# Two of twelve low parts per narrow chunk moved from VectorE to GpSimd, their matmuls one half piece later, and a scatter three half pieces later

## The chip, the cores and the metric

The kernel runs on one core of one Trainium2 chip. The metric is device time in microseconds (us) of one execution. The engines are called as the profile calls them: PE is TensorE's matmuls, PEld its weight loads, DVE is VectorE, ACT is ScalarE, POOL is GpSimd, SP is SyncE, whose queue (SPq) issues the weight loads from memory.

## The reference

A decoder trunk of two layers on 256 tokens of width 1024, all in float32. Layer 0 has latent attention and a dense SwiGLU, layer 1 an mLSTM and then a mixture of experts, in which each token goes to two of eight experts. The last part takes most of the time and is what the change touches:

```python
def swiglu(h, wg, wu, wd):
    return (jax.nn.silu(h @ wg) * (h @ wu)) @ wd

for e in range(N_EXPERTS):            # N_EXPERTS = 8, D_MODEL = 1024, D_FF = 3584
    y = y + combine[..., e:e + 1] * swiglu(h, wg[e], wu[e], wd[e])
```

## The kernel before

**Split numbers.** A float32 weight is used as the sum of a high part and a low part, each in a format that PE multiplies in one pass. `split` (L204) makes both from a loaded tile: ACT casts the weight into `whi` (L221), and the engine passed as `sub`, DVE unless told otherwise, subtracts that from the weight and writes `wlo` (L225). Both inputs of this subtraction, `raw` and `whi`, lie in SBUF. Each of `whi` and `wlo` has four buffers, the loaded tiles `raw` have ten.

**Experts.** The experts are sorted by their number of tokens and dealt to eight places, even ones wide (128 token slots), odd ones narrow (64 slots). In a narrow place the high and low parts of the 64 tokens stand side by side as 128 columns, so each part of a weight is multiplied once (`mm2s`, L242: all `whi` matmuls at L245, then all `wlo` matmuls at L247); in a wide place a half piece takes six matmuls (`mm3s`, L234: L237, L238 with `whi`, L240 with `wlo`). An expert's 3584 hidden columns are worked in seven chunks of 512. `_chunks` lays the chunks of a wide and of a narrow expert alternately, 28 of each.

**Pieces.** A chunk has three weights, each loaded as two pieces of 1 MB, and each piece is split and used in two halves: twelve half pieces, four each of gate, up and down. Below, G0 to G3, U0 to U3 and D0 to D3 are the half pieces of a narrow chunk's gate, up and down. The down pieces of a chunk follow the gate and up pieces of the next chunk. The stream thus repeats: a wide chunk's gate and up (8 half pieces), the narrow chunk's down before it (4), a narrow chunk's gate and up (8), the wide chunk's down (4).

**Order.** `Stream.run` walks the half pieces. Ahead of a half piece's matmuls it splits those up to three further on (`fill`, with AHEAD = 3). `soon(n, f)` (L184) puts off `f` by half pieces: it is called after the matmuls of the n-th half piece, counting the present one when it is called from `use`. PE, DVE and ACT run their instructions in exactly the order in which this code gives them (`in_order`, L453); POOL and SP are not bound by hand. `inner` (L1275) issues the gate and up matmuls of a half piece, `summed` (L1383) closes an expert: it makes `ye_hi` and `ye_lo` of the sum and puts the four scatters (L1459: two matmuls at L1463 and one DVE addition to `xs` at L1466) one and two half pieces later. `one_hot_at` (L1227) runs on POOL once per expert from the second place on, two operations at L1232.

Of the kernel before, what the change touches and what calls it, by code (L numbers as in the profile page):

```python
# [23 lines left out]
KB = D // P  # L24
# [22 lines left out]
WIDE = (True, False, True, False, True, False, True, False)  # L47
# [39 lines left out]
def trunk(ctx: ExitStack, tc: tile.TileContext, out, rope_inv, x, positions, norm_mix, norm_ffn,  # L87
# [3 lines left out]
    nc = tc.nc  # L91
# [35 lines left out]
    def ps(tag, shape, dtype=F32):  # L127
        return psum.tile(shape, dtype, name=uniq("ps_" + tag), tag=tag, bufs=4)


    def load(src, shape, key=None):
        if key in early:
            return early.pop(key)
        n = int(np.prod(shape[1:]))
        t = weights.tile([P, 2048], F32, name=uniq("raw"), tag="raw", bufs=NB_RAW)
        v = t[:, :n]
        if len(shape) == 3:
            v = v.rearrange("p (k c) -> p k c", k=shape[1])
        nc.sync.dma_start(v, src)
        return v  # L140
# [18 lines left out]
    class Stream:  # L159
# [2 lines left out]
        def __init__(self):  # L162
            self.items, self.ready, self.later, self.at = [], [], [], 0

        def piece(self, src, shape, use, after=None, key=None):

            raw = []

            def get(j, sub):
                if not raw:  # L170
                    raw.append(load(None if key in early else src(), shape, key))
                v = raw[0]
                if isinstance(v, list):
                    return [w.rearrange("p a c -> p (a c)") for w in split(v[2 * j:2 * j + 2], sub)]
                return split(v[:, 2 * j:2 * j + 2] if shape[1] == 4 else v[:, j], sub)

            self.items.append((partial(get, 0), lambda w: use(0, w), None))
            self.items.append((partial(get, 1), lambda w: use(1, w), after))
# [25 lines left out]
    def split(v, sub=nc.vector):  # L204
        vs = v if isinstance(v, list) else [v]
        shape = [P, 2, 512] if isinstance(v, list) else list(v.shape)
        n = int(np.prod(shape[1:]))
        hi = weights.tile([P, 1024], F32R, name=uniq("whi"), tag="whi", bufs=NB_HI)[:, :n]
        lo = weights.tile([P, 1024], F32R, name=uniq("wlo"), tag="wlo", bufs=NB_LO)[:, :n]
        if len(shape) == 3:  # L210
            hi = hi.rearrange("p (k c) -> p k c", k=shape[1])
            lo = lo.rearrange("p (k c) -> p k c", k=shape[1])
        if chores and begun[0]:
            chores.pop(0)()
        with ExitStack() as order:
            if held:
                for ins in held.pop(0):
                    order.enter_context(tc.issue_after(ins))
            for i, part in enumerate(vs):
                h, l = (hi[:, i], lo[:, i]) if isinstance(v, list) else (hi, lo)  # L220
                nc.scalar.copy(h, part)  # L221
                if sub == PUT_OFF:
                    put_off.append(partial(nc.vector.tensor_sub, l, part, h.bitcast(F32)))
                elif sub:
                    sub.tensor_sub(l, part, h.bitcast(F32))  # L225
        return hi, lo
# [12 lines left out]
        for o, l, r, _, stop in terms:  # L239
            nc.tensor.matmul(o, l[0], r[1], start=False, stop=stop)  # L240

    def mm2s(terms):  # L242

        for o, l, r, start, _ in terms:
            nc.tensor.matmul(o, l, r[0], start=start, stop=False)  # L245
        for o, l, r, _, stop in terms:
            nc.tensor.matmul(o, l, r[1], start=False, stop=stop)  # L247


    ident = const([P, P], F32, "ident")  # L250
# [100 lines left out]
    def rsqrt_steps(ssq, scales, name):  # L351

        n = ssq.shape[1]
        v = tmp([P, n], F32, name + "_v")
        y = tmp([P, n], F32, name + "_y")
        t = tmp([P, n], F32, name + "_t")
        yi = y.bitcast(I32)
        steps = [partial(nc.vector.tensor_scalar, v[:, a:b], ssq[:, a:b], 1.0 / width, EPS, op0=OP.mult, op1=OP.add)
                 for a, b, width in scales]
        steps += [partial(nc.vector.tensor_scalar, yi, v.bitcast(I32), 1, None, op0=OP.logical_shift_right),  # L360
                  partial(nc.vector.tensor_scalar, yi, yi, -1.0, float(0x5F3759DF), op0=OP.mult, op1=OP.add)]
        each = [slice(i, i + 1) for i in range(n)]
        if n <= NT:
            steps.append(partial(nc.vector.tensor_scalar, v, v, -0.5, None, op0=OP.mult))
        for _ in range(3):
            if n <= NT:
                steps += [partial(nc.vector.scalar_tensor_tensor, t[:, c], y[:, c], v[:, c], y[:, c],
                                  op0=OP.mult, op1=OP.mult) for c in each]
                steps += [partial(nc.vector.scalar_tensor_tensor, y[:, c], t[:, c], 1.5, y[:, c],
                                  op0=OP.add, op1=OP.mult) for c in each]  # L370
            else:
                steps += [partial(nc.vector.scalar_tensor_tensor, t, y, -0.5, y, op0=OP.mult, op1=OP.mult),
                          partial(nc.vector.tensor_mul, t, t, v),
                          partial(nc.vector.scalar_tensor_tensor, y, t, 1.5, y, op0=OP.add, op1=OP.mult)]
        return y, steps
# [71 lines left out]
    def at(pair, *idx):  # L447
        return pair[0][idx], pair[1][idx]
# [158 lines left out]
    r, more = rsqrt_steps(ssq, [(0, NT, Q_LORA), (NT, 2 * NT, KV_LORA)], "lat")  # L607
# [25 lines left out]
    def q_rotary(wq4, b):  # L633
        p = ps("a", [P, 4, ROPE])
        for k in range(2):
            mm3(p, tok(cT, k, b), at(wq4[k], slice(None), slice(None), slice(NOPE, QK)), k == 0, k == 1)
        return p
# [7 lines left out]
    for a in range(2):  # L645
        for b in range(NT):
            nc.tensor.matmul(rows_p[:, a, b * P:(b + 1) * P], r[:, 2 * a + b:2 * a + b + 1].to_broadcast([P, P]), ident,
                             start=True, stop=True)
# [65 lines left out]
    for half in range(2):  # L714
# [6 lines left out]
        for b in range(NT):  # L721
            p = q_rotary(wq4, b) if half else qr_first[b]
# [3 lines left out]
        for h in range(hs, hs + 4, 2):  # L726
            p = ps("a", [P, 2, S])
# [6 lines left out]
        for h in range(hs, hs + 4, 2):  # L734
            p = ps("a", [P, 2, S])
# [3 lines left out]
        for b in range(NT):  # L739
            p = ps("a", [P, 4, VD])  # L740
# [52 lines left out]
    piece = []  # L793
# [60 lines left out]
    r = x_ffn.rsqrt("ffn0")  # L854
# [79 lines left out]
    for k in range(KB):  # L934
        for n in range(2):
            nc.tensor.matmul(rows_p, wg[:, k].rearrange("p a c -> p (a c)"), aT[n][:, k],
                             start=k + n == 0, stop=k == KB - 1 and n == 1)
# [35 lines left out]
    for blocks, src in ((slice(0, 2), Mr), (slice(2, 3), Mr[:, P:])):  # L973
        n = src.shape[1] // P
        src = src.rearrange("p (a c) -> p a c", a=n)
# [43 lines left out]
    for h in range(HEADS):  # L1019
        e = ps("b", [P, 3, P])  # L1020
# [3 lines left out]
                         start=False, stop=True)  # L1024
# [30 lines left out]
    r = rsqrt_pool(hsq, VD, "head")  # L1055
# [159 lines left out]
    def expert_at(n):  # L1215

        if n == 0:
            return 0
        if not numbers:
            numbers.extend(nc.values_load_multi_w_load_instructions(  # L1220
                ids[0:1, :], engines=[nc.sync.engine], min_val=0, max_val=NE - 1,
                skip_runtime_bounds_check_because="a sum of expert numbers of which one alone is taken")[1])
        return numbers[n]
# [22 lines left out]
    for h2 in range(HEADS // 2):  # L1246
        t = ps("a", [P, 2, S])
        y = tmp([P, 2, NT, VD], F32, "y")
        for j in range(2):
            h = 2 * h2 + j  # L1250
# [16 lines left out]
    def expert_chunk(e, c):  # L1267

        for w, after in ((moe_w_gate, gated), (moe_w_up, upped)):
            p = []  # L1270
            for i in range(2):
                moe.piece(lambda w=w, i=i: w[expert_at(e), c, i], [P, 4, 512], partial(inner, e, i, p),
                          partial(after, e, c, p) if i else None)

    def inner(e, i, p, j, w):  # L1275
        if i + j == 0:
            p.append(ps("a", [P, 512]))
        xg = tokens[e][0]
        k = 4 * i + 2 * j
        if not WIDE[e]:  # L1280
            mm2s([(p[0], xg[:, k + kk], at(w, slice(None), kk), k + kk == 0, k + kk == KB - 1) for kk in range(2)])
            return
        mm3s([(p[0], (xg[:, 0, k + kk], xg[:, 1, k + kk]), at(w, slice(None), kk), k + kk == 0, k + kk == KB - 1)
              for kk in range(2)])
# [98 lines left out]
    def summed(e):  # L1383

        ye = []
        for h in range(2):
            hi = tmp([P, 512], F32R, "ye_hi")
            nc.scalar.copy(hi, acc[e, h])
            ye.append([hi])
        for h in range(2):  # L1390
            lo = tmp([P, 512], F32R, "ye_lo")
            nc.vector.tensor_sub(lo, acc[e, h], ye[h][0].bitcast(F32))
            ye[h].append(lo)
        for h in range(2):
            for b in range(NT):
                moe.soon(1 + h, partial(scatter, e, h, b, ye[h]))

    def last_down(e, c):

# [68 lines left out]
    moe = Stream()  # L1468
# [109 lines left out]
    xg = bigt([P, KB, P], F32, "xg")  # L1578
    with tc.If(rv > 0):
        for e in range(NE):  # L1580
# [5 lines left out]
            for c in range(NCH):  # L1586
                gu = []
                for w in (moe_w_gate[e], moe_w_up[e]):
                    p = ps("a", [P, 512])
# [14 lines left out]
                for i in range(2):  # L1604
                    raw = load(moe_w_down[e, 2 * c + i], [P, 2, D])
                    for h in range(2):
                        for kk in range(2):
                            j = 2 * i + kk
                            nc.tensor.matmul(acc[h], hT[:, j], raw[:, kk, h * 512:(h + 1) * 512],
                                             start=c == 0 and j == 0, stop=c == NCH - 1 and j == 3)  # L1610
            for h in range(2):
                ye = tmp([P, 512], F32, "ye_hi")
                nc.scalar.copy(ye, acc[h])
                for b in range(NT):
                    p = ps("a", [P, 512])
# [61 lines left out]
```

## Time and profile before

| | |
|---|---|
| median of 3 runs | 1419.63 us (1419.06 to 1422.76) |
| profiled execution, its own time | 1419.83 us |
| its span in the trace | 1418.1 us |
| granted clock of PE over the span | 0.992 of full speed |
| stretch of the experts in the trace | about 500 to 1390 us |
| busy share of the span | PE 96%, DVE 88%, ACT 70%, POOL 6% |

The span is what the trace covers, from the first instruction to the last; 1.7 us of the profiled execution's time lie around it. Two notes for reading the rows: PE's matmuls overlap, so the shown length of one (about 0.39 us) is longer than the distance from one to the next (0.23 us); and DVE's operations overlap slightly too, so a row of eleven 1.22 us operations is shorter than eleven times that.

### The profile page before, as it was taken

To read this page: it belongs to the slowest core of one execution; us is meant where nothing else is said; L and a number is where in the kernel's file an instruction comes from. 1 tells how busy PE (TensorE), PEld (TensorE's weight loads), DVE (VectorE), ACT (ScalarE), POOL (GpSimd) and SP (SyncE) were. 2 spreads that over 40 slices of the span, in tenths; PEclk is the share of its full clock that TensorE was granted. 3 is DMA by queue.
4 is the path that set the end of the run, shared out by engine and by line. 5 is a ranking of instruction groups with operands and counts; after the bars stand their busy time and mean duration, and the time that the engine had idled before them with its cause. 6 is when DMAs were issued, how large, how long until landed. Compare 5 with 4: busy or idle time off the path is not lost.

```text
span 1418.1 us, 18971 instructions
## 1 busy us (share of the span) xinstructions
PE 1367.2 (96%) x6457; PEld 1090.4 (77%) x6457; DVE 1249.8 (88%) x1602; ACT 998.5 (70%) x1270; POOL 78.2 (6%) x112
## 2 busy tenths in 40 slices
PE   7999999999999899999999999999999999999995
PEld 5888888888887687777777878777777777777774
DVE  6959998957977898989999898999989899999996
ACT  5545444444864587878878787878878787888884
POOL 4300000000020100000000020000011000001000
PEclk9999999999999999999999999999999999999998
DMA  9455666555457598999999999999999998999970
GB/s 359 159 208 208 216 213 210 193 184 207 169 188 267 224 365 311 379 374 369 370 370 399 379 368 372 384 373 358 403 368 388 378 400 341 394 404 398 388 315 32
DMA packets 63183, 439.07 MB, mean 310 GB/s; under 512 B 7441, under 2 KB 7606, under 8 KB 11238
## 3 DMA queue, kind: packets, MB, share of 16 engines
q1 hardware_dynamic: 61190, 429.20, 78.6%
q0 software_dynamic: 1728, 8.56, 1.7%
q8 instruction: 52, 0.85, 0.2%
q14 instruction: 53, 0.43, 0.1%
q10 hardware_dynamic: 160, 0.02, 0.0%
HBM read 436.67 MB, written 1.08 MB: 309 GB/s over the span
## 4 chain that ended last, share of the span: by engine, by line
PE 81%; DVE 12%; issue 3%; ACT 2%; POOL 1%; DMA 0%; DVEq 0%; ACTq 0%; POOLq 0%
PE ps_a L237 11%; PE ps_a L238 11%; PE ps_a L240 11%; PE ps_a L247 7%; DVE wlo L225 6%; PE ps_a L245 4%; PE ps_b L237 4%; PE ps_b L238 4%; PE ps_b L240 4%; PE ps_a L1334 3%; PE ps_b L232 3%; PE ps_b L230 3%; PE ps_b L231 3%; PE ps_b L245 3%; PE ps_b L247 3%
## 5 line engine op out<-in xcount | busy, mean ns | idle before, releaser
L225 DVE TENSOR_TENSOR wlo<-raw,whi 128x1024 fp32r<-128x1024 f32 (+1 forms) x787 | 923.8, 1218 | 97.6 <-ACT whi L221 92.4
L221 ACT CAST whi<-raw 128x1024 fp32r<-128x1024 f32 (+1 forms) x796 | 801.2, 1049 | 252.3 <-PE ps_a L238 95.7
L237 PE MATMUL ps_a<-whi,xg 128*128 128x512 f32 x448 | 177.3, 396 | 1.1 <-ACT whi L221 1.1
L238 PE MATMUL ps_a<-whi,xg 128*128 128x512 f32 x448 | 175.5, 392 | 0.0
L247 PE MATMUL ps_a<-wlo,xg 128*128 128x512 f32 x448 | 153.2, 423 | 11.2 <-DVE wlo L225 11.2
L240 PE MATMUL ps_a<-wlo,xg 128*128 128x512 f32 x448 | 139.6, 393 | 1.9 <-DVE wlo L225 1.9
L245 PE MATMUL ps_a<-whi,xg 128*128 128x512 f32 x448 | 141.1, 396 | 0.0
L247 PEld LDWEIGHTS ps_a<-wlo,xg 128*128 128x128 f32 x448 | 74.5, 189 | 67.5 <-DVE wlo L225 58.6
L240 PEld LDWEIGHTS ps_a<-wlo,xg 128*128 128x128 f32 x448 | 84.0, 188 | 21.7 <-DVE wlo L225 3.2
L237 PEld LDWEIGHTS ps_a<-whi,xg 128*128 128x128 f32 x448 | 84.2, 188 | 20.0 <-ACT whi L221 1.5
L245 PEld LDWEIGHTS ps_a<-whi,xg 128*128 128x128 f32 x448 | 84.2, 189 | 19.3
L238 PEld LDWEIGHTS ps_a<-whi,xg 128*128 128x128 f32 x448 | 84.3, 188 | 18.2 <-DVE xg L1539 0.5
L237 PE MATMUL ps_b<-whi,hT_hi 128*128 128x512 f32 x224 | 90.9, 406 | 0.0
L237 PE MATMUL ps_a<-whi,xT_hi 128*128 128x512 f32 x224 | 88.6, 395 | 0.1
L238 PE MATMUL ps_a<-whi,xT_lo 128*128 128x512 f32 x224 | 88.4, 395 | 0.0
L238 PE MATMUL ps_b<-whi,hT_lo 128*128 128x512 f32 x224 | 88.1, 394 | 0.0
L785 DVE CUSTOM_DVE_ANT_0 junk<-raw,wr 128x1024 bf16<-128x1024 f32 x64 | 78.1, 1220 | 2.5 <-DMA raw<-mlstm_w_out_dram 1.9
L245 PE MATMUL ps_b<-whi,hT_hi 128*128 128x512 f32 x224 | 73.8, 409 | 0.0
L1232 POOL TENSOR_SCALAR oh<-slots,slot_at 128x128 f32<-128x128 f32 x14 | 27.5, 1970 | 815.3 <-PE ps_a L1521 392.1
L247 PE MATMUL ps_b<-wlo,hT_hi 128*128 128x512 f32 x224 | 71.6, 399 | 0.3 <-DVE wlo L225 0.3
L240 PE MATMUL ps_b<-wlo,hT_hi 128*128 128x512 f32 x224 | 70.3, 395 | 0.0
L240 PE MATMUL ps_a<-wlo,xT_hi 128*128 128x512 f32 x224 | 70.1, 393 | 0.0
(444 smaller groups left out, 1941.9 us busy)
## 6 DMA issues: line engine op xcount, KB each, us to landing
raw<-moe_w_gate_dram SPq DMA_DIRECT2D x112, 1024.0 KB, 7.2
raw<-moe_w_up_dram SPq DMA_DIRECT2D x112, 1024.0 KB, 7.3
raw<-moe_w_down_dram SPq DMA_DIRECT2D x107, 1024.0 KB, 7.3
raw<-ffn_w_gate_dram SPq DMA_DIRECT2D x14, 1024.0 KB, 4.9
raw<-ffn_w_up_dram SPq DMA_DIRECT2D x14, 1024.0 KB, 4.7
raw<-ffn_w_down_dram SPq DMA_DIRECT2D x14, 1024.0 KB, 5.0
raw<-mlstm_w_in_dram SPq DMA_DIRECT2D x12, 1024.0 KB, 4.7
raw<-mla_w_out_dram SPq DMA_DIRECT2D x4, 1024.0 KB, 7.8
```

The source lines that it names most:

```text
L221: nc.scalar.copy(h, part)
L225: sub.tensor_sub(l, part, h.bitcast(F32))
L230: nc.tensor.matmul(o, l[0], r[0], start=start, stop=False)
L231: nc.tensor.matmul(o, l[0], r[1], start=False, stop=False)
L232: nc.tensor.matmul(o, l[1], r[0], start=False, stop=stop)
L237: nc.tensor.matmul(o, l[0], r[0], start=start, stop=False)
L238: nc.tensor.matmul(o, l[1], r[0], start=False, stop=False)
L240: nc.tensor.matmul(o, l[0], r[1], start=False, stop=stop)
L245: nc.tensor.matmul(o, l, r[0], start=start, stop=False)
L247: nc.tensor.matmul(o, l, r[1], start=False, stop=stop)
L785: nc.vector.tensor_tensor_reduce(junk, a, b, 1.0, 0.0, OP.mult, OP.add, acc)
L1334: nc.tensor.matmul(t[:, n, j], src[:, j * P:(j + 1) * P], twice, start=n + j == 0, stop=n + j == 4)
```

## The change

For the gate and the up weight of a narrow chunk, the subtraction of the second half piece (G1 and U1) is issued on POOL instead of DVE, through the argument `on_pool`. The low-part matmuls of those two half pieces are put off with `moe.soon(2)`: they run after all matmuls of the next half piece (G2, U2). The four scatters of an expert come four and five half pieces after `summed` instead of one and two.

```diff
-        def piece(self, src, shape, use, after=None, key=None):
+        def piece(self, src, shape, use, after=None, key=None, on_pool=None):
...
             def get(j, sub):
+                if j == on_pool:
+                    sub = nc.gpsimd
...
-    def mm2s(terms):
+    def mm2s(terms, later=None):
 
         for o, l, r, start, _ in terms:
             nc.tensor.matmul(o, l, r[0], start=start, stop=False)
-        for o, l, r, _, stop in terms:
-            nc.tensor.matmul(o, l, r[1], start=False, stop=stop)
+
+        def low_parts():
+            for o, l, r, _, stop in terms:
+                nc.tensor.matmul(o, l, r[1], start=False, stop=stop)
+
+        later(low_parts) if later else low_parts()
...
-                          partial(after, e, c, p) if i else None)
+                          partial(after, e, c, p) if i else None, on_pool=None if WIDE[e] or i else 1)
...
-            mm2s([(p[0], xg[:, k + kk], at(w, slice(None), kk), k + kk == 0, k + kk == KB - 1) for kk in range(2)])
+
+            mm2s([(p[0], xg[:, k + kk], at(w, slice(None), kk), k + kk == 0, k + kk == KB - 1) for kk in range(2)],
+                 partial(moe.soon, 2) if (i, j) == (0, 1) else None)
...
-                moe.soon(1 + h, partial(scatter, e, h, b, ye[h]))
+                moe.soon(4 + h, partial(scatter, e, h, b, ye[h]))
```

## Rows read from the trace of the kernel before

**Rows 1.** The page, part 1: busy us, share of the span, instructions

```profile
PE 1367.2 (96%) x6457; PEld 1090.4 (77%) x6457; DVE 1249.8 (88%) x1602; ACT 998.5 (70%) x1270; POOL 78.2 (6%) x112
```

**Rows 2.** Busy time by stretch, the experts: engines, PE clock, DMA share, GB/s

```profile
500.00:1390.00 890.00, 872.38 (x4041) 688.80 (x4040) 828.16 (x822) 726.09 (x846) 28.01 (x15) 1.00 0.95 371
```

**Rows 3.** Waits, 500 to 1390: engine, line, releaser: total us, times, longest

```profile
PEld ps_a L247 <- DVE wlo L225: 58.6, 126, 1.1
ACT whi L221 <- PE ps_b L238: 53.0, 27, 2.1
DVE wlo L225 <- ACT whi L221: 43.7, 62, 1.2
PE ps_a L247 <- DVE wlo L225: 11.2, 26, 0.6
PEld ps_a L1463 <- DVE ye_lo L1392: 8.2, 6, 2.3
```

**Rows 4.** Waits of the DMA queue itself, 500 to 1390

```profile
SPq L139 <- DVE wlo L225: 696.2, 311, 6.4
```

**Rows 5.** Chain that ended last, 911 to 925: start us, us, what

```profile
911.00 0.47 PE ps_b L245 x2
911.47 0.46 PE ps_b L247 x2
...
920.74 0.47 PE ps_a L245 x2
921.21 0.66 PE ps_a L247 x2
...
924.14 0.23 PE ps_b L237
```

**Rows 6.** Timeline of DVE, 880 to 970: start us, us, operation, count, [idle before]

```profile
912.46 4.62 DVE L225 TENSOR_TENSOR wlo<-raw,whi 128x1024 fp32r<-128x1024 f32 x4
917.00 0.69 DVE L1360 TENSOR_TENSOR hT_lo<-ps_a,hT_hi 128x512 fp32r<-128x512 f32 x1
917.60 12.57 DVE L225 TENSOR_TENSOR wlo<-raw,whi 128x1024 fp32r<-128x1024 f32 x11
930.76 1.23 DVE L225 TENSOR_TENSOR wlo<-raw,whi 128x1024 fp32r<-128x1024 f32 x1 [0.59 <-ACT whi L221]
...
951.28 1.28 DVE L1392 TENSOR_TENSOR ye_lo<-ps_b,ye_hi 128x512 fp32r<-128x512 f32 x2
...
957.38 10.52 DVE L225 TENSOR_TENSOR wlo<-raw,whi 128x1024 fp32r<-128x1024 f32 x9
968.64 1.22 DVE L225 TENSOR_TENSOR wlo<-raw,whi 128x1024 fp32r<-128x1024 f32 x1 [0.73 <-ACT whi L221]
```

**Rows 7.** Timeline of ACT, 908 to 932

```profile
910.58 2.95 ACT L221 CAST whi<-raw 128x1024 fp32r<-128x1024 f32 x3 [0.30 <-PE ps_a L238]
```

**Rows 8.** Timeline of POOL, first 60 us: the two subtractions of 1024 columns

```profile
24.41 2.34 POOL L616 TENSOR_TENSOR wlo<-raw,whi 128x1024 fp32r<-128x1024 f32 x1
41.02 2.41 POOL L225 TENSOR_TENSOR wlo<-raw,whi 128x1024 fp32r<-128x1024 f32 x1
```

**Rows 9.** Timeline of DVE beside these, and line 495's lengths (ns min/median/max)

```profile
24.47 2.30 DVE L533 SCALAR_TENSOR_TENSOR mix_y<-mix_t,mix_y 128x1 f32<-128x1 f32 x1
41.33 0.67 DVE L731 TENSOR_TENSOR qkT<-ps_a,rows 128x512 f32<-128x512 f32 x1
41.93 1.65 DVE L495 TENSOR_TENSOR qr<-rope_u,rope_v 128x128 f32<-128x128 f32 x1
...
L495 DVE TENSOR_TENSOR qr<-rope_u,rope_v x8: 279/280/1803, 38.0 to 51.9; 128x128 f32<-128x128 f32 x8
```

**Rows 10.** Timeline of POOL and of DVE, 814 to 818, in the experts' stretch

```profile
814.69 2.31 POOL L1232 TENSOR_SCALAR oh<-slots,slot_at 128x128 f32<-128x128 f32 x1 [188.96 <-PE ps_a L1521]
814.26 1.22 DVE L225 TENSOR_TENSOR wlo<-raw,whi 128x1024 fp32r<-128x1024 f32 x1
815.39 2.45 DVE L225 TENSOR_TENSOR wlo<-raw,whi 128x1024 fp32r<-128x1024 f32 x2
```

## The prediction

> **What bounds the kernel now.** The page's busy shares come first [rows 1]: PE 96%, DVE 88%, POOL 6%. They suggest that DVE work could go to POOL for nothing, and that PE would then hardly gain. Shares over the span mix stages, so the second view is the stretch of the experts alone [rows 2]: in 890 us PE shows 872 busy (its matmuls overlap, so this is too high), DVE 828, and the DMA engines are busy 95% of the time. Third come the waits there [rows 3]: PE's low-part matmuls of the narrow chunks (L247) wait for DVE's `wlo` 126 times at the weight load and 26 times at the matmul, some 152 waits in 28 narrow chunks, over five in each; DVE waits for ACT's casts 43.7 us, and ACT itself waits for PE to free buffers. No wait for a DMA is among them. The DMA queue, on the other side, waits for DVE to free loaded tiles [rows 4]: loading follows the compute and doesn't limit it.
>
> So the bound changes within a pair of chunks. The chain [rows 5] shows it: a narrow half piece that PE runs freely takes 0.47 + 0.46 = 0.93 us (911.00, 911.47), but in the gate and up of the next chunk 0.47 + 0.66 = 1.13 us (920.74, 921.21), which is DVE's pace: eleven `wlo` in a row take 12.57 us, so (12.57 - 1.22) / 10 = 1.135 us from one to the next [rows 6]. There DVE has no idle time: from 912.46 to 930.17 it runs 4 `wlo`, one `hT_lo` and 11 `wlo` without a gap [rows 6]; its next idle time is 0.59 us, in the wide part, where a half piece has six matmuls and PE leads. **In the narrow gate and up DVE sets the pace; DVE's idle time lies elsewhere, and with only three half pieces split ahead it can't be used for the narrow part.** Whatever DVE's queue loses or gains between G0 and U3 reaches the end of the run nearly one to one, 28 times.
>
> **The change, part by part.**
>
> *Removed from DVE.* 2 x 28 = 56 subtractions, each worth a distance of 1.135 us on a full queue: 2.27 us a chunk, 63.6 us in all.
>
> *Added on POOL.* 56 subtractions of 1024 columns. The trace has two on POOL: 2.34 and 2.41 us [rows 8]. POOL is free in that stretch (28 us of 890, [rows 2]), so their length alone would cost nothing as long as PE gets the result in time.
>
> *What they do to DVE.* This decides, and the trace shows it in the first 60 us. Beside POOL's subtraction at 24.41 to 26.75, DVE's operation on a single column starts at 24.47 and takes 2.30 us: it ends when POOL's ends [rows 8, 9]. Beside the one at 41.02 to 43.43, L495 starts at 41.93 and takes 1.65 us, where its median is 0.28 [rows 9]; it too ends just behind POOL's. Between them L731, one of whose inputs is in PSUM, runs in 0.67 us under the same POOL operation. So a DVE operation with both inputs in SBUF stands still while POOL subtracts two SBUF tiles. Nearly all that DVE runs between G0 and U3 is `wlo<-raw,whi`, of just this kind; only `hT_lo` (0.60 us, an input from PSUM) isn't.
>
> *Who comes first.* Against a running DVE queue POOL waits: its operation at 814.69 begins under a `wlo`, takes 2.31 us, and ends 0.4 us behind the second `wlo`'s end (about 816.6), while DVE's pair from 815.39 takes 2.45 us, 0.1 more than two at the usual distance [rows 10]. I read this as: POOL is let in after the operation in flight and one more. G1's cast, the third of three from 910.58, ends at 913.53 [rows 7], when D3's subtraction is in flight (the first of four from 912.46); POOL would get in behind G0's at about 914.8, hold DVE until 917.1, and G2's `wlo` follows. U1's turn comes behind U0's in the same way; its buffer comes free only when G1's put-off low matmuls are done, which still leaves PE three half pieces.
>
> *Price.* A hold costs DVE 2.30 us [rows 9] and saves 1.135: **+1.16 us each, 2.33 a chunk, +65 us for 28.** Bounds: if G1's request falls one operation later, `hT_lo` runs under the hold and G1 costs 0.56 instead of 1.16, together 1.72 a chunk, +48 us; the longest hold, 2.41 plus the 0.1 of rows 10 for the hand-over, gives 1.37 each, +77 us. Below zero lies only the case without a hold (a rival). I take the full price, since both requests, placed by the rows, find DVE with `wlo` next.
>
> *Put-off low matmuls.* The same matmuls in another order, no cost by themselves. They keep a `wlo` buffer one half piece longer: the split four places on waits for them. For G1 that is U1 on POOL, for U1 the second half piece of the wide down on DVE. Behind that one on DVE the next `wlo` would queue, but DVE reaches it two operations after U3, when PE, at DVE's pace, has done U1. Without that cover the cost is up to one matmul group, 0.47 us a chunk (13 us in all); I take 0. PE's own need: G1's low matmuls come after G2, and G2's `wlo` on DVE is later than POOL's result, so PE waits for DVE, not for POOL.
>
> *Scatter later.* It removes PE's waits for `ye_lo` (8.2 us at six weight loads, [rows 3]). These stand behind the three narrow experts that end mid-stream. DVE there is full from `ye_lo` at 951.28 to 967.90, with its next idle time at 968.64 [rows 6], and the additions at L1466 stay in the same narrow gate and up. PE waits less for `ye_lo` and as much more for the next `wlo`. Gain between 0 and 8 us; I take 1, as DVE's full queue is the nearest row. The same move at the wide experts falls in PE's part and adds or removes no instruction: 0.
>
> *DMA and POOL's queue.* SP reloads a tile when its second half is subtracted, for the two first pieces now by POOL, some 2 to 4 us later. Ten tiles and no wait for a DMA cover this: 0. Two one-hot operations per expert share POOL's queue in one narrow chunk of seven, up to 2.3 us each [rows 10]; if they came ahead of U1, its result would be late there by up to 4.6 us in at most 4 chunks: 0 to 18 us, taken as 0, because U1's subtraction is given before them.
>
> *Sum.* 1419.83 (the profiled execution: span 1418.1 and 1.7 around it; 0.2 above the median) + 65 - 1 = **1484 us**, with 1464 (+48, -4) to 1497 (+77) for this case. PE's clock stays at 1.00 in this stretch, as PE remains busy.
>
> **The rivals.** *A, no hold for long subtractions.* The held operations seen in rows 9 are short; a pair of two 1024-column subtractions side by side is not in the trace. If DVE ran on beside POOL, it would be 2.27 us ahead per chunk, and PE's loss in the narrow part would go: four half pieces at 0.2 us (1.13 less 0.93) and some 0.6 us at the first wait, 1.4 us a chunk, 39 us: **1381 us, faster**. It decides as soon as the hold is below 1.135 us. Against it: both operations of the right kind in rows 9 end with POOL's. Chance 0.10.
>
> *B, partly covered holds.* If both holds regularly fall on a DVE operation with a PSUM input, of the size of `hT_lo` (0.60 us from its start to the next), 1.20 of the 2.33 us is covered: 1.13 x 28 = 32 us, **1450 us** (1440 to 1464, above which the forecast's own lower bound takes over). Against it: between G0 and U3 there is one such operation, and none near U1. Chance 0.08.
>
> *C, POOL is let in only when DVE pauses.* DVE would run G2, G3, U0 and U2 first. G3 starts at 917.60 in rows 6, so U2 ends at 917.60 + 3 x 1.135 + 1.22 = 922.22, less two subtractions that are gone, 919.95. There DVE must stop for a buffer, POOL runs until 922.3, and PE has stood since G2. Then PE does G1's low part (0.47), G3, U0 (0.93 each), U1's high part, U2, U1's low part and U3: U3 ends at 927.4 instead of 924.14 [rows 5], 3.3 us x 28 = 92: **1512 us**. Against it: in rows 10 POOL got in between back-to-back operations. Chance 0.06.
> The Trainium skill ("SBUF — State Buffer", section "Who interferes with whom") bears on A and C: it says that a DVE instruction with two SBUF inputs and a POOL instruction that reads SBUF exclude each other for the whole instruction, and that the order of issue decides who blocks. By that rule the trace agrees against A (2.30 us held of 2.34); for C it leaves open how long DVE's queue keeps the first place, and rows 10 alone speak.
>
> *The change does nothing* (holds just equal what they save, 1.135 us): within 4 us of 1419.8, chance 0.02.
>
> **How the numbers follow.** Forecast 0.74, A 0.10, B 0.08, C 0.06, nothing 0.02. The range takes in the forecast's bounds, B below and C's time above: 1440 to 1512, leaving out A, the null case and part of C, some 0.15. About 0.3% (4 us) is what a measurement of this kernel can tell from no change: faster 0.10, same 0.02, slower 0.88.
>
> **What would show it.** In the changed trace: POOL with 56 subtractions of 2.3 us or, with their wait for DVE, up to 4.5 us; in every narrow chunk two DVE `wlo` (G2 and U0 or U2) of up to 3.4 us instead of 1.22; PE's waits for `wlo` at L247 grown by some 60 us; DVE's idle time unchanged in sum (890 - 828 = 62 us, [rows 2]), nearly all of it in the wide parts; a pair of chunks 2.3 us longer. I am wrong if DVE's `wlo` keep 1.22 us beside POOL's (A), or if PE waits for POOL rather than DVE (C).

## The result, and the profile of the changed kernel

The changed kernel takes 1503.47 us (median of 4 runs, 1501.3 to 1506.14), the kernel before 1419.49 us: a ratio of 1.0587, 95% interval 1.0561 to 1.0614, or 84 us more. The forecast was 1484 us with a range of 1440 to 1512. The profiled execution took 1506.14 us, its span is 1504.4 us.

The page, part 1 (busy us, share of the span, instructions), against [rows 1]; then busy time by stretch, the experts, which now reach to about 1475 us, against [rows 2] (columns as there: PE, PEld, DVE, ACT, POOL, PE clock, DMA share, GB/s):

```profile
PE 1375.0 (91%) x6457; PEld 1106.1 (74%) x6457; DVE 1301.6 (87%) x1546; ACT 1005.3 (67%) x1270; POOL 245.5 (16%) x168
```

```profile
500.00:1475.00 975.00, 880.75 (x4033) 705.15 (x4031) 878.98 (x766) 731.92 (x845) 195.16 (x71) 0.98 0.92 339
```

DVE has 56 instructions fewer and POOL 56 more, as the change says. Yet DVE's busy time in the experts went up from 828 to 879 us (from 1249.8 to 1301.6 over the whole span): DVE has fewer operations, and some of them take longer. PE's clock there is 0.98 on the mean, where it was 1.00. The first 500 us are the same in both.

The waits of the same stretch, against [rows 3], and those of the DMA queue, against [rows 4]:

```profile
PEld ps_a L251 <- DVE wlo L227: 121.1, 77, 3.3
PE ps_a L251 <- DVE wlo L227: 87.1, 51, 2.9
DVE wlo L227 <- ACT whi L223: 75.1, 80, 3.1
PEld ps_a L251 <- POOL wlo L227: 4.1, 2, 2.1
```

```profile
SPq L139 <- DVE wlo L227: 719.2, 312, 6.4
SPq L139 <- POOL wlo L227: 65.4, 28, 4.2
```

(L225 and L247 of before are L227 and L251 here.) PE waits for DVE fewer times but far longer: 121.1 us at the weight loads where it was 58.6, 87.1 at the matmuls where it was 11.2. It hardly waits for POOL, twice in 56. SP waits 28 times for POOL to free a loaded tile; no engine's wait for a DMA is among the long ones.

What POOL does to DVE is seen in one narrow chunk. First POOL's timeline, then DVE's, operation by operation (start us, us), against [rows 6]:

```profile
1063.00 3.43 POOL L227 TENSOR_TENSOR wlo<-raw,whi 128x1024 fp32r<-128x1024 f32 x1 [25.60 <-ACT whi L223]
1068.44 3.04 POOL L227 TENSOR_TENSOR wlo<-raw,whi 128x1024 fp32r<-128x1024 f32 x1 [2.01 <-PE ps_a L251]
```

```profile
1064.23 3.30 DVE L227 TENSOR_TENSOR wlo<-raw,whi 128x1024 fp32r<-128x1024 f32 x1
1067.44 0.68 DVE L1368 TENSOR_TENSOR hT_lo<-ps_a,hT_hi 128x512 fp32r<-128x512 f32 x1
1068.05 1.21 DVE L227 TENSOR_TENSOR wlo<-raw,whi 128x1024 fp32r<-128x1024 f32 x1
1069.18 3.39 DVE L227 TENSOR_TENSOR wlo<-raw,whi 128x1024 fp32r<-128x1024 f32 x1
1072.49 4.62 DVE L227 TENSOR_TENSOR wlo<-raw,whi 128x1024 fp32r<-128x1024 f32 x4
```

These are G2 (3.30), `hT_lo`, G3 (1.21), U0 (3.39) and, in the last row, U2, U3 and two of the wide down. G2 begins at 1064.23, stands until POOL's G1 ends at 1066.43, and ends 1.10 us behind that; U0 likewise behind POOL's U1 (1071.48). Each is some 2.1 to 2.17 us longer than the usual 1.22. PE beside it, against [rows 5]:

```profile
1067.58 1.19 PE L251 MATMUL ps_a<-wlo,xg 128*128 128x512 f32 x4 [1.20 <-DVE wlo L227]
...
1072.62 0.72 PE L251 MATMUL ps_a<-wlo,xg 128*128 128x512 f32 x2 [2.11 <-DVE wlo L227]
1073.18 1.10 PE L247 MATMUL ps_a<-whi,xg 128*128 128x512 f32 x4
1074.11 1.10 PE L251 MATMUL ps_a<-wlo,xg 128*128 128x512 f32 x4
1075.05 0.63 PE L247 MATMUL ps_a<-whi,xg 128*128 128x512 f32 x2
1075.51 0.63 PE L251 MATMUL ps_a<-wlo,xg 128*128 128x512 f32 x2
1075.98 0.40 PE L239 MATMUL ps_b<-whi,hT_hi 128*128 128x512 f32 x1
```

The rows show two pauses, 1.20 us at G2 and 2.11 us at U0, both ended by the DVE operation that was held. From U0 on PE doesn't wait any more in this chunk. U1's subtraction holds U0 in 22 of the 28 narrow chunks of the trace.

### The profile page after: what moved, and what is told of

The parts are those of the page before. It is cut to its first block, busy times and chain, and to the rows that moved or that the text cites. A ratio compares the mean times of both kernels' runs of the same rounds, so it can differ in the third digit from the quotient of the medians.

```text
span 1504.4 us, 19073 instructions
## 1 busy us (share of the span) xinstructions
PE 1375.0 (91%) x6457; PEld 1106.1 (74%) x6457; DVE 1301.6 (87%) x1546; ACT 1005.3 (67%) x1270; POOL 245.5 (16%) x168
## 4 chain that ended last, share of the span: by engine, by line
PE 73%; DVE 15%; issue 5%; ACT 5%; POOL 1%; DMA 0%; DVEq 0%; ACTq 0%; POOLq 0%
DVE wlo L227 10%; PE ps_a L239 10%; PE ps_a L240 10%; PE ps_a L242 10%; PE ps_a L251 5%; PE ps_b L239 4%; ACT whi L223 3%; PE ps_a L247 3%; PE ps_b L242 3%; PE ps_b L240 3%; PE ps_a L1342 3%; PE ps_b L234 3%; PE ps_b L232 3%; PE ps_b L233 3%; PE ps_b L247 2%
## 5 line engine op out<-in xcount | busy, mean ns | idle before, releaser
L227 DVE TENSOR_TENSOR wlo<-raw,whi 128x1024 fp32r<-128x1024 f32 (+1 forms) x731 | 973.7, 1368 | 133.6 <-ACT whi L223 125.7
L227 POOL TENSOR_TENSOR wlo<-raw,whi 128x1024 fp32r<-128x1024 f32 (+2 forms) x62 | 180.7, 2916 | 667.4 <-ACT whi L223 570.4
L251 PE MATMUL ps_a<-wlo,xg 128*128 128x512 f32 x448 | 149.8, 438 | 91.7 <-DVE wlo L227 87.1
L251 PEld LDWEIGHTS ps_a<-wlo,xg 128*128 128x128 f32 x448 | 85.2, 205 | 140.2 <-DVE wlo L227 121.1
L242 PE MATMUL ps_a<-wlo,xg 128*128 128x512 f32 x448 | 139.4, 392 | 1.9 <-DVE wlo L227 1.9
L247 PE MATMUL ps_a<-whi,xg 128*128 128x512 f32 x448 | 140.8, 417 | 0.0
L247 PEld LDWEIGHTS ps_a<-whi,xg 128*128 128x128 f32 x448 | 89.6, 201 | 21.4
L242 PEld LDWEIGHTS ps_a<-wlo,xg 128*128 128x128 f32 x448 | 83.9, 188 | 21.7 <-DVE wlo L227 3.2
L239 PEld LDWEIGHTS ps_a<-whi,xg 128*128 128x128 f32 x448 | 84.2, 188 | 19.7 <-ACT whi L223 1.5
L240 PEld LDWEIGHTS ps_a<-whi,xg 128*128 128x128 f32 x448 | 84.2, 188 | 18.4 <-DVE xg L1547 0.5
L247 PE MATMUL ps_b<-whi,hT_hi 128*128 128x512 f32 x224 | 73.3, 407 | 0.0
L251 PE MATMUL ps_b<-wlo,hT_hi 128*128 128x512 f32 x224 | 71.0, 396 | 1.3 <-DVE wlo L227 1.3
```

Of the source, the lines that this page charges most:

```text
L239: nc.tensor.matmul(o, l[0], r[0], start=start, stop=False)
L240: nc.tensor.matmul(o, l[1], r[0], start=False, stop=False)
```

## The experiments

The theory: a POOL subtraction stops DVE's subtractions for its length, which costs time where DVE sets PE's pace. The rivals: POOL's result is late, the put-off matmuls carry the loss, or something else follows from the longer pauses.

**Take away POOL's reading (e4_write_only).** The low part of G1 and U1 is left out: POOL writes zeros instead.

```diff
...
+                elif sub is nc.gpsimd and begun_moe[0]:
+                    for _ in range(3):
+                        sub.memset(l.bitcast(F32), 0.0)
...
```

> POOL makes no subtraction for G1 and U1 but writes zeros into the same low-part tile, three times over, so it is busy about as long but reads nothing from SBUF; the low part of these half pieces is left out. Theory (DVE stands still because both engines read SBUF): no DVE subtraction over 1.4 us, DVE is ahead by two subtractions per chunk, PE's waits at the narrow low parts all but vanish, and the time falls below that of the kernel before, to about 1380 us (1370 to 1395). Rival (POOL's result is late, or the put-off matmuls and their buffers cost): time stays above 1460 us, with PE waiting for POOL.

Measured: 1387.34 us, ratio to before 0.9769 (0.9753 to 0.9785). POOL's and DVE's operations in its trace (DVE: ns min/median/max):

```profile
L229 POOL MEMSET wlo<- 128x1024 f32 x168 | 160.5, 956 | 553.0 <-PE ps_b L255 439.2 <-PE ps_a L255 46.5 <-PE ps_b L246 36.6
...
L231 DVE TENSOR_TENSOR wlo<-raw,whi x587: 1210/1220/1228, 500.8 to 1362.7; 128x1024 fp32r<-128x1024 f32 x196
```

POOL is as busy there, 160 us, but no DVE subtraction exceeds 1.228 us. 116 us separate this kernel from the changed one, and 32 us of it lie below the kernel before: I read this as what DVE's pace in the narrow chunks costs there, at the least, as the put-off is still in this kernel. It isn't a gain to keep, because the kernel leaves out 56 low parts. The memsets don't wait for ACT's cast as the subtractions do, so POOL is also earlier; since PE hardly waited for POOL in the changed kernel, that isn't where the 116 us come from. The Trainium skill ("SBUF — State Buffer", section "Who interferes with whom") says that a DVE instruction with two SBUF inputs contends with a POOL instruction that reads SBUF, not with one that only writes it; the rows of the changed kernel (3.30 and 3.39 us) agree with the first half, the rows here (at most 1.228 us) with the second.

**Move the holds to where DVE has time (e9_wide_instead).** One POOL subtraction in each wide chunk, none in the narrow ones, nothing put off, the scatter as before.

```diff
-    ... on_pool=None if WIDE[e] or i else 1)
+    ... on_pool=1 if WIDE[e] and not i and w is moe_w_up else None)
...
```

> The kernel before with one subtraction per wide chunk on POOL (the second half piece of the up weight), none in the narrow chunks, no put-off matmuls, the scatter as before. Theory (a hold costs time only where DVE sets the pace; in the wide part DVE has 1.7 to 2.2 us idle per pair, more than the 1.03 a hold costs it): 1416 to 1430 us, in spite of 28 holds of about 2.2 us. Rival (a hold costs its 0.8 to 0.95 us wherever it is): 1442 to 1447 us.

Measured: 1425.61 us, ratio 1.0036 (1.0023 to 1.0049). A subtraction in POOL's timeline there, and the one beside it in DVE's:

```profile
1043.28 2.40 POOL L227 TENSOR_TENSOR wlo<-raw,whi 128x1024 fp32r<-128x1024 f32 x1 [29.04 <-ACT whi L223]
1044.53 2.23 DVE L227 TENSOR_TENSOR wlo<-raw,whi 128x1024 fp32r<-128x1024 f32 x1 [1.21 <-ACT whi L223]
```

POOL starts 1.25 us ahead of DVE, while DVE waits for a cast. So DVE's operation is only 1.0 us longer than the usual 1.22, not the 2.2 us that I expected, and the move saves DVE 1.135 us: its busy time over the span is 1249.4 us, against 1249.8 before. The 28 subtractions cost 5 us here; one per narrow chunk costs 29 to 33 us, as the next two runs show. What this run shows is that a POOL subtraction that begins in DVE's idle time costs little. What a full hold of 2.1 us would cost in the wide part isn't shown, nor where the 5 us come from.

**One at a time (e5_gate_alone, e8_up_alone).** G1 alone, then U1 alone on POOL; both low parts stay put off and the scatter late.

```diff
-    ... on_pool=None if WIDE[e] or i else 1)
+    ... on_pool=None if WIDE[e] or i or w is moe_w_up else 1)      # e5_gate_alone
+    ... on_pool=None if WIDE[e] or i or w is moe_w_gate else 1)    # e8_up_alone
```

> The changed kernel with only G1 on POOL, U1 back on DVE. Theory: one hold of 2.17 us for a saved 1.135 at G2, after which PE follows DVE through U3, so no further loss: 1.03 us x 28 = 29 us, and few falls of PE's clock since the long pause of 2.3 us at U0 is gone: 1446 to 1456 us. Rival (every hold costs the same share of the whole loss): half of 84, 1462 us.

> The changed kernel with only U1 on POOL, G1 back on DVE. Theory: the hold at U0 costs 1.03 us, PE then runs the rest of the up weight at its own pace behind DVE, 0.55 us more, and PE's clock falls in some chunks: 1.58 us x 28 = 44, with up to 1.5 us for each fall: 1460 to 1480 us, above the gate alone by 10 to 30 us. Rival (the holds cost alike): within 5 us of the gate alone.

Measured: 1452.75 us (ratio 1.0238, 1.0221 to 1.0255) and 1448.70 us (1.0212, 1.0195 to 1.0229), so 33 and 29 us. The first lies in the theory's span. The second missed it (1460 to 1480) and is within 5 us of the first, as the rival said. The trace shows why: U1's hold fell elsewhere. POOL and DVE in that kernel, one narrow chunk:

```profile
1035.54 5.00 POOL L227 TENSOR_TENSOR wlo<-raw,whi 128x1024 fp32r<-128x1024 f32 x1 [27.48 <-ACT whi L223]
```

```profile
1035.96 2.35 DVE L227 TENSOR_TENSOR wlo<-raw,whi 128x1024 fp32r<-128x1024 f32 x2
1038.44 3.19 DVE L227 TENSOR_TENSOR wlo<-raw,whi 128x1024 fp32r<-128x1024 f32 x1
```

U0 and U2 went ahead of POOL, and U3 was held: POOL's operation took 5.00 us, 2.6 of it waiting. PE beside it, and its waits for POOL between 500 and 1420 us:

```profile
1040.60 0.73 PE L251 MATMUL ps_a<-wlo,xg 128*128 128x512 f32 x2 [1.23 <-POOL wlo L227]
```

```profile
PE ps_a L251 <- POOL wlo L227: 24.0, 20, 1.3
```

These are U1's put-off low matmuls, with only U3 behind them. So here PE waits for POOL's late result, the first rival of this section, 20 times and in spite of the put-off. Together the two singles cost 62 us; both contain the put-off of both low parts (7 us, next run), so 56 us without counting it twice, if the prices add. The changed kernel costs 84: **28 us come only from the two together**.

**The put-off alone (e2_defer_only).** DVE makes all low parts; G1's and U1's low matmuls are put off; scatter as before.

```diff
-    ... on_pool=None if WIDE[e] or i else 1)
+    ... on_pool=None)
...
-                moe.soon(4 + h, partial(scatter, e, h, b, ye[h]))
+                moe.soon(1 + h, partial(scatter, e, h, b, ye[h]))
```

> The kernel before with the put-off low matmuls of G1 and U1 alone; DVE makes all low parts, the scatter stays. Theory: the order of matmuls and the longer-held buffer cost little: 1419 to 1430 us. Rival (the put-off matmuls carry the loss): 1450 us or more.

Measured: 1426.41 us, ratio 1.0054 (1.0037 to 1.0071): 7 us, inside the theory's span.

```profile
1027.83 1.19 PE L251 MATMUL ps_a<-wlo,xg 128*128 128x512 f32 x4 [0.60 <-DVE wlo L227]
1028.86 0.63 PE L247 MATMUL ps_a<-whi,xg 128*128 128x512 f32 x2
1029.32 0.64 PE L251 MATMUL ps_a<-wlo,xg 128*128 128x512 f32 x2
```

```profile
1023.16 9.16 DVE L227 TENSOR_TENSOR wlo<-raw,whi 128x1024 fp32r<-128x1024 f32 x8
```

Behind U2's `wlo` PE has U2's and U1's low matmuls and then U3 to do, at its own pace, to 1029.79, 1.96 us from the end of its wait. In the kernel before only U2's low matmuls lay there, and U3 followed at DVE's pace, 1.135 us plus the last 0.66 us. DVE's row begins with G3 and U0 to U3, so U3 is done at 1023.16 + 4 x 1.135 + 1.22 = 1028.92, and PE ends U3's matmuls 1.04 us behind that (1029.96), where it was 0.77 before (923.37 to 924.14, [rows 5, 6]). The difference, 0.27 us a chunk, makes the 7 us.

**The change without the put-off (e12_no_put_off).**

```diff
-                 partial(moe.soon, 2) if (i, j) == (0, 1) else None)
+                 None)
```

> The changed kernel without the put-off: POOL makes G1's and U1's low parts, their matmuls come at once, the scatter stays late. Theory (POOL's result is there before the subtraction that DVE was held in, so the put-off buys nothing and costs 0.3 to 0.55 us a chunk at the end of the up weight): 8 to 15 us below the changed kernel, 1488 to 1496 us. Rival (POOL's result is late for PE, which the put-off hides): 1510 us or more, with PE waiting for POOL.

Measured: 1505.61 us, ratio to before 1.0597 (1.058 to 1.0615). Neither expectation held. PE now does wait for POOL, and PE's clock is lower still (0.96 over the stretch):

```profile
PEld ps_a L251 <- POOL wlo L227: 28.3, 25, 3.0
```

```profile
500.00:1480.00 980.00, 895.13 (x4045) 716.02 (x4044) 877.05 (x767) 729.79 (x847) 182.65 (x71) 0.96 0.89 337
```

So POOL's result is late for an immediate use, in 25 chunks, and the put-off hides it; but PE reaches the same held DVE operation anyway, and the time is the same. That isn't proof that the put-off costs nothing here: PE's clock falls to 0.50 at 21 places of the experts in this trace and at 13 in the changed kernel's, so two different sums come out alike.

**PE's clock (e6_pe_kept_busy, e10_pe_kept_busy_half).** The mean of 0.98 in the changed kernel is made of 13 short falls of 3.4 us each; the kernel before has one in the experts. Three stretches of its trace, and PE's timeline there:

```profile
1172.00:1184.50 12.50, 9.21 (x40) 6.61 (x39) 12.06 (x9) 10.04 (x13) 5.70 (x2) 1.00 0.94 335
1184.50:1187.90 3.40, 3.40 (x9) 2.65 (x9) 3.40 (x4) 1.83 (x2) 0.00 (x0) 0.50 0.90 366
1187.90:1192.00 4.10, 4.10 (x25) 3.52 (x25) 3.05 (x3) 3.43 (x4) 0.00 (x0) 1.00 1.00 396
```

```profile
1183.05 0.72 PE L251 MATMUL ps_a<-wlo,xg 128*128 128x512 f32 x2 [2.11 <-DVE wlo L227]
1183.61 1.21 PE L247 MATMUL ps_a<-whi,xg 128*128 128x512 f32 x4
1184.61 1.91 PE L251 MATMUL ps_a<-wlo,xg 128*128 128x512 f32 x4
...
1187.96 0.40 PE L239 MATMUL ps_b<-whi,hT_hi 128*128 128x512 f32 x1
```

Behind the pause of 2.11 us the granted clock falls to 0.50, the 1.2 GHz level; four matmuls that took 1.10 us in the chunk shown first take 1.91, and by 1187.90 the clock is back at 2.4 GHz. From U0's low matmuls to the wide chunk's first matmul PE takes 4.91 us here (1183.05 to 1187.96) and 3.36 us in the chunk shown first (1072.62 to 1075.98): a fall costs about 1.55 us, and the twelve more than before some 18 us, by estimate. The two kernels put matmuls of zeros into PE's pauses, which add nothing to the sums:

```diff
+            if (i, j) == ((0, 0) if up else (1, 0)):
+                def busy_then(low_parts):
+                    for _ in range(8 if up else 4):
+                        nc.tensor.matmul(p[0][:N], zerob, onesb[:, None, :].to_broadcast([P, 4, P]), start=False, stop=False)
+                    low_parts()
+                mm2s(terms, busy_then)
...
-                    for _ in range(8 if up else 4):
+                    for _ in range(4 if up else 2):      # e10_pe_kept_busy_half
```

> The changed kernel with matmuls of zeros put where PE pauses in the narrow chunk: 4 of 512 columns (bf16, 64 output rows) between G2's high and low parts, 8 between U0's, about 0.9 and 1.8 us of PE time, less than the pauses of 1.2 and 2.3 us. Theory (PE's clock falls after the pauses, 13 times in the experts' stretch, at about 1.2 to 1.6 us each): the clock stays up there and the time falls by 15 to 22 us, to 1481 to 1489 us. Rival (the clock's fall costs nothing, the holds alone make up the loss): unchanged within 4 us, or slower by what the added matmuls cost.

> The changed kernel with half as many matmuls of zeros in PE's pauses, 2 between G2's high and low parts and 4 between U0's. Theory (a fall of PE's clock costs 1 to 1.7 us, and the added matmuls of the fuller version cost some of what they saved): clock above 0.988 and 1488 to 1496 us. Rival (the falls cost little, about 5 us in all): 1497 to 1502 us whatever the clock.

Measured: 1497.99 us with the full number (ratio to before 1.0553, 1.0532 to 1.0575) and 1491.86 us with half of it (1.0509, 1.0492 to 1.0525); the mean clock is 0.99 in both, where the changed kernel has 0.98. The full version gave less than expected, 5 us below the changed kernel; the half one gave 12 us and lies in the theory's span. Their traces have one fall and two (one of them 6.8 us long) left in the experts. That the added matmuls of the full version cost what they saved is not shown: its profiled execution, at a clock of 0.993, took 1494.33 us, and the three others, at 0.992 to 0.987, took 1497.48 to 1501.72. So in this version the longer executions are those with the lower clock. **The falls cost 12 us of the 84 by e10, which leaves some in, and about 18 by the rows.**

**The scatter (e3_no_scatter_move, e1_scatter_only).** The changed kernel without the move, and the move alone.

```diff
-                moe.soon(1 + h, partial(scatter, e, h, b, ye[h]))
+                moe.soon(4 + h, partial(scatter, e, h, b, ye[h]))      # e1_scatter_only; e3 is the reverse
```

> The changed kernel with the scatters back at one and two half pieces. Theory: the move is worth little, 1503 to 1512 us. Rival (the move is needed since POOL's holds and the scatter collide): over 1512 us.

> The kernel before with the scatters three half pieces later, nothing else. Theory: DVE is full at these places, PE's wait for the sum's low part turns into waits for DVE's next subtractions: 1415 to 1420 us. Rival (PE's waits of 14.5 us there are real losses): 1405 to 1411 us.

Measured: 1503.67 us, no different from the changed kernel, and 1417.70 us, ratio 0.9983 (0.9973 to 0.9994), 2 us below before.

**Lead (e7_four_ahead, e11_five_ahead).** If the narrow chunks are bound by DVE for want of lead, more lead must help the kernel before, without POOL. (The kernel gives each number a line of its own.)

```diff
-NB_RAW, NB_HI, NB_LO, AHEAD = 10, 4, 4, 3
+NB_RAW, NB_HI, NB_LO, AHEAD = 9, 5, 5, 4        # e7_four_ahead
+NB_RAW, NB_HI, NB_LO, AHEAD = 8, 6, 6, 5        # e11_five_ahead
```

> The kernel before with five buffers each for high and low parts instead of four, half pieces split four ahead instead of three, and nine loaded tiles instead of ten; no subtraction on POOL. Theory (DVE's idle time in the wide part can't be used because it may run only three half pieces ahead): one half piece more lets DVE enter the narrow part 1.1 us further ahead, PE's loss of 1.4 us a chunk falls by about 1 us: 1385 to 1400 us. Rival (the loss isn't one of lead, or nine tiles are too few to hide the loads): 1415 us or more.

> The kernel before with six buffers each for high and low parts, five half pieces split ahead, and eight loaded tiles. Theory (lead is what the narrow part lacks; four ahead left 0.3 us of 1.4 a chunk): a further 5 to 12 us below four ahead, 1381 to 1389 us. Rival (eight loaded tiles are too few to cover the loads, or what is left isn't lead): 1391 us or more, and with too few tiles ACT waits for a DMA.

Measured: 1393.26 us, ratio 0.9805 (0.9789 to 0.9821), and 1391.92 us, 0.9801 (0.9786 to 0.9816). With four ahead PE's wait at the narrow low parts is

```profile
PEld ps_a L247 <- DVE wlo L225: 18.0, 58, 0.4
```

where it was 58.6 us; with five it is gone from the list, yet the time falls by 1 us only, less than I expected, and no wait for a DMA shows up. Four ahead takes nearly all that these two steps of lead give. Both beat both kernels.

## Why the prediction was right in kind and 20 us low

**The range: right by some luck.** The forecast's own bounds end at 1497 us, below the 1503 measured. The range reached 1512 to cover rival C, which is not what happened in the changed kernel. Kind, sign and main cost came true; two further costs were put at nothing.

**The bound: right.** DVE sets PE's pace in the narrow gate and up, and what is done to its queue there reaches the end: e4 shows it, e7 too (27 us less with more lead), and e9 agrees but holds DVE for less.

**The hold: right, over-priced.** G2 and U0 were held for 2.1 to 2.17 us. The 2.30 us of [rows 9] was the whole length of a held operation, its own work included; its line in the trace of the kernel before (ns min/median/max) gives 0.148 us for that, so the same row already said 2.15:

```profile
L533 DVE SCALAR_TENSOR_TENSOR mix_y<-mix_t,mix_y x6: 145/148/2300, 17.0 to 26.7; 128x1 f32<-128x1 f32 x6
```

A hold as in the chunk shown costs about 1.03 us net and not 1.16. A few chunks are held for less, and DVE's busy time over the span rose by 51.8 us: I take 52 us, where 65 was forecast. That the rows of the first 60 us, with operations of 1 and 128 columns, would hold for pairs of 1024 columns was the main risk, rival A; the rows of 3.30 and 3.39 us rule it out. Rival B is out as well: `hT_lo` runs behind the held G2, not under POOL. Rival C, POOL let in only at a pause of DVE, isn't what happened in the changed kernel, where G2 and U0 are held; but in e8 U1 comes close to it (two subtractions ahead of POOL, and PE waiting for POOL).

**Who comes first: the step that failed.** From [rows 10] I read that POOL is let in after the operation in flight and one more, which lets U1 in behind U0. In the changed kernel it came in ahead of U0, right behind G3, the operation in flight. That moves PE's pause from U2 to U0, and with it a cost I had not counted: behind its pause PE has 3.5 half pieces left in the weight, which it runs at its own 0.93 us, while DVE's next subtractions are early and wait for nothing. U3's matmuls end at 1076.14, 1.30 us behind DVE's U3 (1072.49 + 1.135 + 1.21 = 1074.84); before, they ended 0.77 us behind it. That is 0.53 us a chunk, 15 us; but 0.27 of it is there with the put-off alone (e2), so some 0.26 us a chunk, 7 us, is left for U0's place.

**PE's clock: the other step that failed.** The prediction said that the clock stays at 1.00 since PE remains busy. With a pause of 2.11 us in most narrow chunks the clock fell to 0.50 in 13 places, and matmuls put into the pauses took most of the falls away: worth 12 us by e10, some 18 by the rows. In the singles the pauses are shorter or lie later, and their clock is 0.99 over the span as before's.

**The sum now.** 52 (holds) + 7 (put-off) + 7 (U0's place) + 18 (clock) = 84 us, as measured. This is an estimate: the first is the growth of DVE's busy time, the second e2's time, the third comes from one chunk's rows and the last from two chunks', so each is good to a few us, and that the sum comes out so closely is partly luck. What the singles lack (28) is then U0's place, most of the clock's falls, and a few us of holds: DVE's busy time rose by 22.2 and 22.9 us in the singles and by 51.8 in the changed kernel.

**Put-off: sized wrongly.** I took 0 with a bound of 13 us; alone it costs 7. With POOL on, it hides waits for POOL (e12), and the time is the same without it, with more falls of the clock. My reason, that PE waits for DVE rather than for POOL, holds in the changed kernel, and fails without the put-off and in e8.

**Scatter: right.** -1 us forecast, -2 alone, 0 in the change.

**DMA and POOL's queue: right.** SP waits for POOL 28 times, 65.4 us in all, and nobody waits for a DMA because of it.

**Signs.** PE's waits for `wlo` grew by 62.5 us at the weight loads, as forecast (60), and by 75.9 at the matmuls; the two rows are not to be added, since a pause can show in both. DVE's idle time didn't stay at 62 us but grew to 975 - 879 = 96. I read this as PE, late behind U0, letting DVE run into its limit of three half pieces again; no run shows it.

## What to carry to other kernels

Before moving work to an idle engine, look in the trace for a place where the two engines already ran side by side, and read what the busy one's operations took there: two rows of 2.30 and 1.65 us decided this case. What such a subtraction costs hangs on where it falls: 28 of them cost 5 us where they began in DVE's idle time, and 29 to 33 in the narrow chunks, where DVE sets the pace. Where two engines take turns as the bound, one more buffer of lead (27 us here) was worth more than any move of work tried here, and a pause put into the steady engine can cost its clock as well.

## What the runs showed of the hardware that I had not expected

Which DVE operation a POOL subtraction stops isn't fixed by the distance between them that the rows show: asked 0.39 us behind a subtraction's start, POOL got in before the next one (1068.44 in the changed kernel); asked 0.71 us behind it, it let two more pass (1035.54 in e8) and came in at a gap of 0.13 us in DVE's queue; asked 0.82 us behind it (885.87 behind 885.05 in the changed kernel), it again got in before the next, which took 3.40 us:

```profile
885.87 2.63 POOL L227 TENSOR_TENSOR wlo<-raw,whi 128x1024 fp32r<-128x1024 f32 x1 [3.56 <-ACT whi L223]
```

```profile
885.05 1.21 DVE L227 TENSOR_TENSOR wlo<-raw,whi 128x1024 fp32r<-128x1024 f32 x1
886.18 3.40 DVE L227 TENSOR_TENSOR wlo<-raw,whi 128x1024 fp32r<-128x1024 f32 x1
```

What decides it stays open. PE's clock fell to 0.50 at 1184.50, 1.45 us behind a pause of 2.11 us; behind the same pause at 1072.62 it didn't fall. And a POOL operation that only writes, however busy it keeps POOL (160 us), left DVE's two-input subtractions at 1.22 us throughout.
